# Half-product pairs of a gate/up stage extended to product 5 and to the first down part, with buffers handed out by hand

## The chip, the cores and the metric

One Trainium2 chip, one core of it. The metric is the device time of one execution in microseconds (us). The time of the kernel before is the median of three runs, 1880.92 us (1879.19 to 1881.81). One further execution was recorded by the hardware profiler: it took 1882.15 us, of which 1880.4 us lie between the first and the last instruction (the span). All rows of the profile and of the trace come from that execution.

## What is computed

One layer of a hybrid decoder, on 1024 prompt rows and 8 sample rows (1032 tokens together), in float32: an input projection, three branches (a gated linear recurrence, sliding-window attention, attention into 256 memory tokens), gates that merge them, an output projection, and at the end

```
h = layer_norm(ALPHA * x + merged @ w_out, ln1_g, ln1_b)
gt, up = jnp.split(h @ w_gate_up, 2, axis=-1)
h = layer_norm(ALPHA * h + (jax.nn.silu(gt) * up) @ w_down, ln2_g, ln2_b)
```

with D_MODEL 1024 and an inner width of 2816, which is 22 blocks of 128. The change lies in the last two lines: `h @ w_gate_up` (22 gate blocks and 22 up blocks) and the first part of the product with `w_down`.

## The kernel before, in words

**Products.** Every float32 matrix is split into a high and a low part, hi = the value rounded to the fast matmul type, lo = the rest. A matmul of two such matrices is three matmuls on TensorE: high by high, low rows by high weights, high rows by low weights (L285, L286, L287 in `fast_product`). Weights are 128x128 blocks, the moving rows are 258 tokens wide (a quarter of 1032).

**Units of seven products.** A *unit* makes 256 output columns (for the gate stage one gate block and one up block, for the down stage two row blocks) for all 1032 tokens by a Strassen scheme in its Winograd form: seven products of quarter-size matrices, numbered 0 to 6, in place of eight. Each product needs a weight sum (`fast_quarter`: an addition on VectorE at L269 for products 1, 2, 4 and 5, then the high part by a copy on ScalarE, L84, and the low part by a subtraction on VectorE, L85), and an operand sum of the activations (`ts`, made once for all units). `fast_step` issues one product: for each of two quarter columns p it has 4 k-blocks x 3 = 12 matmuls, so 24 for a product and 168 for a unit, and then takes the sums out of the banks (PSUM): products 0, 1 and 2 by ScalarE copies into small tiles (p1s, p5s, u2s; L320), products 3, 4, 5 and 6 by VectorE additions into the unit's two results za and zb (L325, L327, L330; in the down units product 6 by a ScalarE copy, L1864). Products 0, 2, 4 and 6 of a quarter column add up in one bank b, products 1 and 5 in d, so that the next product may go into the bank only when the copy of the running sum has been made.

**Units in pairs.** The gate stage has 20 units (columns 2 to 21; 0 and 1 are done in another way), taken in pairs (u, v). In the first nine pairs product 3 of both units is not made as a full product: product 3 of two units has the same operand, so that the two together are one matrix product, which is again made by seven *half products* p0, p1, p4 and p6 (p0, p1 and p4 hold two each; `second_quarter`, `second_step`). They cost 7 x 6 = 42 matmuls in place of 2 x 24 = 48, and use operand sums t2 that `second_combos` makes during the first pair. Their banks are pb, pc and pd.

**Order.** `gate_up_down` writes one list of steps, gate units first, then two *down parts* of four units each (units are named fg2 to fg21, f00 to f03, f10 to f13). Weight preparation runs three steps ahead of the products. The scheduler keeps, on each engine, an order that follows from this list, so an instruction that waits holds up all that stands behind it on its engine. The operands of a down part are loaded in the last unit of the stage before it (`down_operand`: operand i+1 after step i; it takes a free z slot, loads from the scratch f or t in DRAM, and splits into the tile that an operand of the stage before has left).

**Buffers.** Results za, zb, G, operand sums and loads for row sums are 128x1032 tiles of one pool z (10 slots, waits decided by the pool in turn); raw weights use 6 tiles, weight sums 4, split weights 5 high and 4 low. A finished gate unit is multiplied into a tile G and stored to scratch f by SP's queue; a finished down unit is added to scratch h in DRAM by two accumulating DMAs from GpSimd's queue (POOL, L1868), and its z slots are free when they have landed.

Of the kernel before, what the change touches and what calls it, by code (L numbers as in the profile page):

```python
# [60 lines left out]
class Builder:  # L61
# [124 lines left out]

    def zt(self, name):
        return self.z.tile([P, T], F32, tag="z", name=name, bufs=self.zbufs)
# [47 lines left out]
    def pair_load(self, u, st, src0, src1, other=None):  # L236

        h = D // 2
        raw = lambda j, e, src: self.half_raw(src[:, e * h:(e + 1) * h], h, f"ur{u}_{j}{e}")
        if other is not None:  # L240
            a11, a12, a21, a22 = (raw(j, e, src) for j, src in enumerate((src0, src1)) for e in range(2))
            st["second"] = raw(2, 1, other)
        else:
            a11, a21, a22, a12 = raw(0, 0, src0), raw(1, 0, src1), raw(1, 1, src1), raw(0, 1, src0)
        return {"raw": [[a11, a12], [a21, a22]], "u": u}
# [51 lines left out]
    def fast_step(self, st, i, ts, finish):  # L297
# [9 lines left out]
        for p in range(2):  # L307
# [10 lines left out]
            if i in (0, 1, 2):  # L318
# [16 lines left out]
        if st.get("pd") is not None and i == 0:  # L335
            nc.vector.scalar_tensor_tensor(st["s", 0, 1], st["pd"]["p", 1], 1.0, st["s", 0, 1], op0=ALU.mult,
                                           op1=ALU.subtract)
# [908 lines left out]
    def h_combos(self, h, ts):  # L1246
# [9 lines left out]
        for p in range(2):  # L1256
            b11, b21, b12, b22 = self.R[p, 0], self.R[p, 1], self.R[2 + p, 0], self.R[2 + p, 1]
            t1 = self.zt(f"ht1_{p}").rearrange("p (k n) -> p k n", k=4)
            tt(t1, b11, b12, ALU.subtract)
            keep(1, p, t1)  # L1260
            yield
# [6 lines left out]
            keep(6, p, b11)  # L1268
            yield
# [743 lines left out]
```

## Time and profile before

| what | value |
|---|---|
| median of three runs | 1880.92 us (1879.19 to 1881.81) |
| profiled execution | 1882.15 us, span 1880.4 us |
| mean granted TensorE clock | 0.997 |
| DVE (VectorE) busy | 1396.7 us, 74% |
| ACT (ScalarE) busy | 1058.6 us, 56% |
| DMA, mean | 164 GB/s, 308.14 MB moved |
| first gate pair fg2/fg3 | starts at 1237.6 us |

PE is TensorE, DVE VectorE, ACT ScalarE, POOL GpSimd, SP the engine that issues most DMAs. "Busy" is the time in which at least one instruction of an engine is recorded; the recorded durations of neighbours may overlap, so that what an instruction costs its engine is the distance from its start to the next one's.

### The profile page before, as it was taken

What the parts mean: (1) busy time and instruction counts of PE and PEld (TensorE: products, weight loads), DVE (VectorE), ACT (ScalarE), POOL (GpSimd) and SP (SyncE); (2) the same over time, 40 slices, a digit from 0 to 9 for tenths busy, and PEclk for the clock granted to TensorE, in tenths of its full rate; (3) what the DMA queues carried; (4) which work ended last, traced back from release to release, by engine and by line L of the source; (5) the groups of instructions that cost most, each with busy time, mean ns of one, the idle gap of its engine ahead of it and who ended that gap; (6) DMA issues with size and microseconds to landing.
All of it is one profiled execution on the core that took longest, in us unless ns stands there. A gap on an engine that the chain in (4) does not pass through costs nothing.

```text
span 1880.4 us, 37977 instructions
## 1 busy us (share of the span) xinstructions
PE 1861.4 (99%) x14670; PEld 1846.0 (98%) x14670; DVE 1396.7 (74%) x2807; ACT 1058.6 (56%) x2264; POOL 125.0 (7%) x187
## 2 busy tenths in 40 slices
PE   9999999999999999999999999999999999999998
PEld 9999999999999999999999999999999999999998
DVE  7878878888788757568787567786677667858486
ACT  6576676665666756568774234544444444635454
POOL 1001002110000000021210000000000000001100
PEclk9999999999999999999999999999999999999998
DMA  9535345447344368647535251224355345758872
GB/s 329 175 117 174 108 145 167 137 139 267 117 160 164 120 198 267 213 128 238 170 103 189 91 192 57 69 88 146 123 182 201 95 152 194 260 139 266 173 212 91
DMA packets 182213, 308.14 MB, mean 164 GB/s; under 512 B 19264, under 2 KB 97040, under 8 KB 182032
## 3 DMA queue, kind: packets, MB, share of 16 engines
q1 hardware_dynamic: 174928, 286.08, 45.9%
q0 software_dynamic: 4224, 14.78, 4.0%
q10 hardware_dynamic: 2880, 4.85, 0.7%
q8 instruction: 115, 1.88, 0.4%
q14 instruction: 66, 0.54, 0.1%
HBM read 222.10 MB, written 87.73 MB: 165 GB/s over the span
## 4 chain that ended last, share of the span: by engine, by line
PE 89%; DVE 5%; ACT 2%; DMA 2%; issue 1%; SPq 0%; POOL 0%; ACTq 0%; DVEq 0%
PE ub L285 5%; PE ub L287 5%; PE ub L286 5%; PE ubfg L286 4%; PE ubfg L287 4%; PE ubfg L285 4%; PE ud L287 2%; PE ud L286 2%; PE ud L285 2%; PE udfg L287 2%; PE udfg L285 2%; PE udfg L286 2%; PE ubf L285 2%; PE op L130 2%; PE ubf L286 2%; PE op L132 2%
## 5 line engine op out<-in xcount | busy, mean ns | idle before, releaser
L285 PE MATMUL ub<-th,u_6h 128*128 128x258 f32 x240 | 68.5, 285 | 2.7 <-DVE sq L966 1.4
L285 PE MATMUL ub<-th,u_2h 128*128 128x258 f32 x240 | 68.1, 284 | 0.7 <-ACT p1s L320 0.7
L285 PE MATMUL ub<-th,u_4h 128*128 128x258 f32 x240 | 68.2, 284 | 0.3 <-ACT u2s L320 0.3
L287 PE MATMUL ud<-th,u_5l 128*128 128x258 f32 x240 | 68.1, 284 | 0.0
L285 PE MATMUL ud<-th,u_5h 128*128 128x258 f32 x240 | 68.1, 284 | 0.0
L285 PE MATMUL ub<-th,u_0h 128*128 128x258 f32 x240 | 68.1, 284 | 0.0
L287 PE MATMUL ub<-th,u_6l 128*128 128x258 f32 x240 | 68.1, 284 | 0.0
L287 PE MATMUL ud<-th,u_1l 128*128 128x258 f32 x240 | 68.1, 284 | 0.0
L287 PE MATMUL ub<-th,u_4l 128*128 128x258 f32 x240 | 68.0, 284 | 0.0
L287 PE MATMUL ub<-th,u_2l 128*128 128x258 f32 x240 | 68.0, 284 | 0.0
L287 PE MATMUL ub<-th,u_0l 128*128 128x258 f32 x240 | 68.0, 283 | 0.0
L285 PE MATMUL uc<-th,u_3h 128*128 128x258 f32 x240 | 68.0, 283 | 0.0
L285 PE MATMUL ud<-th,u_1h 128*128 128x258 f32 x240 | 68.0, 283 | 0.0
L287 PE MATMUL uc<-th,u_3l 128*128 128x258 f32 x240 | 68.0, 283 | 0.0
L286 PE MATMUL ub<-tl,u_6h 128*128 128x258 f32 x240 | 67.7, 282 | 0.0
L286 PE MATMUL ub<-tl,u_0h 128*128 128x258 f32 x240 | 67.6, 282 | 0.0
L286 PE MATMUL ud<-tl,u_5h 128*128 128x258 f32 x240 | 67.6, 282 | 0.0
L286 PE MATMUL ud<-tl,u_1h 128*128 128x258 f32 x240 | 67.6, 282 | 0.0
L286 PE MATMUL ub<-tl,u_4h 128*128 128x258 f32 x240 | 67.6, 282 | 0.0
L286 PE MATMUL ub<-tl,u_2h 128*128 128x258 f32 x240 | 67.6, 282 | 0.0
L286 PE MATMUL uc<-tl,u_3h 128*128 128x258 f32 x240 | 67.6, 282 | 0.0
L130 PE MATMUL op<-mh,woh 128*128 128x258 f32 x224 | 63.4, 283 | 0.0
(1034 smaller groups left out, 8207.2 us busy)
## 6 DMA issues: line engine op xcount, KB each, us to landing
ur<-win SPq DMA_DIRECT2D x120, 256.0 KB, 3.4
urfg<-wgu SPq DMA_DIRECT2D x89, 256.0 KB, 3.0
scr_f<-G SPq DMA_DIRECT2D x22, 516.0 KB, 2.8
f<-scr_f SPq DMA_DIRECT2D x16, 516.0 KB, 4.0
fs<-scr_t SPq DMA_DIRECT2D x16, 516.0 KB, 5.1
dck<-cmk SPq DMA_DIRECT2D x32, 256.0 KB, 4.6
dcv<-cmvT SPq DMA_DIRECT2D x32, 256.0 KB, 4.6
urf<-wdn SPq DMA_DIRECT2D x32, 256.0 KB, 3.1
```

The costliest lines, as they stand in the source:

```text
L130: nc.tensor.matmul(ps, sh, mh, start=opens and i == 0, stop=False)
L132: self.last_mm = nc.tensor.matmul(ps, sl, mh, start=False, stop=closes and i == last).ins
L285: mm(sh[:, w], xh, start=opens and k == 0, stop=False)
L286: mm(sh[:, w], xl, start=False, stop=False)
L287: self.last_mm = mm(sl[:, w], xh, start=False, stop=k == 3).ins
```

## The change

- **More pairs with half products for product 3.** All ten gate pairs and the two pairs of the first down part now replace product 3 of both units by p0, p1, p4, p6 (twelve pairs, before nine). The operand sums for the down part are made by `down_sums`, kept in a new scratch t2 and loaded by `second_load`.
- **Product 5 in the same way, in the first nine gate pairs** ("fifth"): product 5 of both units becomes the half products v0, v1, v4 and v6. Their operand sums are made once (`fifth_combos`), stored to a new scratch t5 and loaded again in every pair (four loads of 516 KB into two buffers, `fifth_load`). v4 and v6 of a pair are issued inside the next pair, behind its product 0 and product 1.
- **Order in a pair.** In a fifth pair p4 stands straight behind (v, 0), and p6 behind (v, 1); before, p4 stood behind (v, 1) and p6 behind (v, 4). In fifth units the running sum of product 2 goes into za by a VectorE addition in place of the ScalarE copy u2s.
- **Buffers by hand.** z slots (8 in this stage, 10 around it), raw weight tiles and sum tiles are handed out from queues and put back when the program is done with them; a raw load is issued when a tile is put back. G is made in place in za.
- **Down operands.** `down_operand` now runs with operand i after step i (before, i+1), into the tile of the operand with the same number (`home = i`), and puts its z slot back at once.

The core of the diff:

```diff
-        order, cut = [], 2 * ((NF - 2 - PLAIN) // 2)
+        where = {u: n for n, u in enumerate(units)}
+        pairs = [n for n in range(0, len(units), 2) if units[n][0] != FAST - 1]
+        second = {units[n + e] for n in pairs for e in range(2)}
+        fifth = [n for n in pairs if units[n + 1][0] == "g" and units[n + 1][1] < NF - 1]
+        order, tail = [], []
         for n in range(0, len(units), 2):
-            steps = [(units[n + e], i) for e in range(2) for i in range(7)]
-            if n < cut:
-                u, v = units[n:n + 2]
-                steps = [(u, 0), (u, 1), (u, "p0"), (u, 2), (u, 4), (u, "p1"), (u, 5), (u, 6),
+            u, v = units[n:n + 2]
+            if n in fifth:
+                steps = [(u, 2), (u, "p0"), (u, 4), (u, "p1"), (u, 6), (v, 0), (v, "p4"), (v, 1), (v, "p6"), (v, 2),
+                         (v, "v0"), (v, 4), (v, "v1"), (v, 6)]
+            elif u in second:
+                steps = [(u, 2), (u, "p0"), (u, 4), (u, "p1"), (u, 5), (u, 6),
                          (v, 0), (v, 1), (v, "p4"), (v, 2), (v, 4), (v, "p6"), (v, 5), (v, 6)]
-            order += steps
+            else:
+                steps = [(u, i) for i in range(2, 7)] + [(v, i) for i in range(7)]
+            order += [(u, 0)] + tail[:1] + [(u, 1)] + tail[1:] + steps
+            tail = [(v, "v4"), (v, "v6")] if n in fifth else []
...
-        sums, seconds = deque(), self.second_combos()
+        sums, seconds = deque(), chain(self.second_combos([self.R[p, 1] for p in range(2)]), self.fifth_combos())
...
+            if where[u] // 2 * 2 in fifth and where[u] % 2:
+                for j in {0: (1,), "p4": (2,), "v1": (4, 6)}.get(i, ()):
+                    self.fifth_load(j)
...
-                if u[1] == last[u[0]][1] - 1 and i == 3:
-                    self.down_operand(nxt, 0, moving[nxt])
-                if u == last[u[0]] and i < 6:
-                    while sums:
-                        for _ in sums.popleft():
-                            pass
-                    self.down_operand(nxt, i + 1, moving[nxt])
+            if nxt < FAST and u == last[u[0]]:
...
+                if i == "p6":
+                    self.down_operand(nxt, 3, moving[nxt])
+                    if nxt < FAST - 1:
+                        self.second_load(nxt)
+                elif i == "v4":
+                    self.down_operand(nxt, 5, moving[nxt])
+                elif not isinstance(i, str):
+                    self.down_operand(nxt, i, moving[nxt])
```

```diff
+    def fifth_combos(self):
...
+        def put(j, src, sign=1.0):
+            t = self.zt(f"t5{j}")
+            pair = t.bitcast(F32R)[:, :2 * QN], t.bitcast(F32R)[:, 2 * QN:]
+            (self.split if sign > 0 else partial(self.split_scaled, scale=sign))(*pair, src)
+            nc.sync.dma_start(self.scr["t5"][:, (1, 2, 4, 6).index(j), :], t)
+            self.zfree(t)
...
+    def fifth_step(self, su, sv, j, ts, fu, fv):
...
+            z, sign = {0: (za[:, 0], 1.0), 3: (za[:, 0], 1.0), 2: (za[:, 1], 1.0), 5: (za[:, 1], 1.0), 1: (zb[:, 1], -1.0),
+                       4: (zb[:, 1], -1.0), 6: (zb[:, 0], -1.0)}[i]
+            stt(z, ps, sign, z, op0=ALU.mult, op1=ALU.add)
```

Three places in the engines' orders follow. L numbers of the changed kernel are its own (L302 is L269 of before, L328 to L330 are L285 to L287, L367 is L320, L374 is L327, L383 is L336).

VectorE in the first gate pair, before: from the first split of an operand sum (t2l3) to the low weights of product 1 of unit fg2 (ufg2_1l). R are activations, usfg2 weight sums.

```order
L85 TENSOR_TENSOR t2l30_16605<-R11_15174,t2h30_16604 128x516
L1317 TENSOR_TENSOR R01_14872<-R11_15174,R01_14872 128x516
L1287 TENSOR_TENSOR G1_16303<-ft1_3_16509,fu1_3_16511 128x258
L85 TENSOR_TENSOR t2l20_16603<-R11_15174,t2h20_16602 128x516
L269 TENSOR_TENSOR usfg2_1_16556<-urfg2_10_16546,urfg2_11_16548 128x512
L96 SCALAR_TENSOR_TENSOR t2l20_16603<-R01_14872,t2h20_16602 128x516
L269 TENSOR_TENSOR usfg2_2_16566<-usfg2_1_16556,urfg2_00_16542 128x512
L85 TENSOR_TENSOR ufg2_1l_16559<-usfg2_1_16556,ufg2_1h_16558 128x512
```

The same stretch of the changed kernel; z are slots (z2 holds the first sum for product 5), s0 to s2 sum tiles, raw0 to raw2 raw weights.

```order
L85 TENSOR_TENSOR t2l30_16609<-z3_14869,t2h30_16608 128x516
L1338 TENSOR_TENSOR z9_14878<-ft1_3_16509,fu1_3_16511 128x258
L85 TENSOR_TENSOR t2l20_16607<-z3_14869,t2h20_16606 128x516
L1369 TENSOR_TENSOR z1_14867<-z3_14869,z1_14867 128x516
L1394 TENSOR_TENSOR z7_14873<-z5_14871,z7_14873 128x516
L1374 TENSOR_TENSOR z1_14867<-z1_14867 128x516
L96 SCALAR_TENSOR_TENSOR t2l20_16607<-z1_14867,t2h20_16606 128x516
L85 TENSOR_TENSOR z2_14868<-z7_14873,z2_14868 128x516
L302 TENSOR_TENSOR s0_16542<-raw1_16547,raw2_16548 128x512
L302 TENSOR_TENSOR s2_16544<-raw0_16546,raw1_16547 128x512
L302 TENSOR_TENSOR s1_16543<-s0_16542,raw0_16546 128x512
L85 TENSOR_TENSOR ufg2_1l_16564<-s0_16542,ufg2_1h_16563 128x512
```

Four rows more stand between the two, and a fifth (L1393, 128x516) stands ahead of the low weights of product 0, where before there was none; the weight sum of product 1 is now the fourth row from the end.

VectorE around p4, before (pair fg6/fg7; L336 reads bank pd, L1380 and L1382 take p4 out):

```order
L85 TENSOR_TENSOR ufg6_p4l_17826<-usfg6_p1_17682,ufg6_p4h_17825 128x512
L269 TENSOR_TENSOR usfg8_2_18107<-usfg8_1_18040,urfg8_00_17892 128x512
L85 TENSOR_TENSOR ufg7_2l_17858<-usfg7_2_17855,ufg7_2h_17857 128x512
L269 TENSOR_TENSOR usfg7_2_17855<-usfg7_2_17855,urfg7_01_17641 128x512
L85 TENSOR_TENSOR ufg7_4l_17907<-usfg7_4_17904,ufg7_4h_17906 128x512
L336 SCALAR_TENSOR_TENSOR p1sfg7_1_17889<-pdfg6_17693,p1sfg7_1_17889 128x258
L269 TENSOR_TENSOR usfg8_4_18153<-urfg8_00_17892,urfg8_10_17896 128x512
L85 TENSOR_TENSOR ufg6_p6l_17941<-urfg7_01_17641,ufg6_p6h_17940 128x256
L1380 SCALAR_TENSOR_TENSOR zafg7_17950<-pbfg6_17691,p1sfg7_1_17889 128x258
```

In the changed kernel (pair fg4/fg5; L383, L1537 and L1539 are the same three operations):

```order
L85 TENSOR_TENSOR ufg5_1l_17284<-s1_16543,ufg5_1h_17283 128x512
L85 TENSOR_TENSOR ufg4_p6l_17314<-raw4_16550,ufg4_p6h_17313 128x256
L85 TENSOR_TENSOR ufg5_2l_17353<-s3_16545,ufg5_2h_17352 128x512
L302 TENSOR_TENSOR s3_16545<-s3_16545,raw4_16550 128x512
L383 SCALAR_TENSOR_TENSOR p1sfg5_1_17345<-pdfg4_17219,p1sfg5_1_17345 128x258
L1421 TENSOR_TENSOR s1_16543<-s3_16545 128x256
L1537 SCALAR_TENSOR_TENSOR z2_14868<-pbfg4_17217,p1sfg5_1_17345 128x258
```

The reader of pd now stands two rows behind the low weights of (v, 2), with p4 due straight behind (v, 0); on TensorE the scheduler puts 6 to 10 matmuls of (v, 1) between the first and the second product of p4.

SP's queue around the load of operand 3 of the second down part, before; the waits are the semaphores of the row (DMASW are those of GpSimd's accumulating DMAs; 2 and 3 belong to unit f01, 4 and 5 to unit f02).

```order
L1429 DMA fs120_22587<-scr_t_80 128x1032 [waits DMAHW3_49,DMASW0_49]
L1429 DMA fs121_22593<-scr_t_80 128x1032 [waits DMAHW4_49,DMASW1_49]
L1391 DMA f1TrueFalse0_22632<-scr_f_79 128x4x258 [waits DMAHW5_49,DMASW2_49]
L1391 DMA f1TrueFalse1_22638<-scr_f_79 128x4x258 [waits DMAHW6_49,DMASW3_49]
L105 DMA urf11_00_22844<-wdn 128x512 [waits DMAHW7_49,DVE_49]
```

The changed kernel; operand 3's second half is the load into z3.

```order
L1610 DMA z0_14866<-scr_t_80 128x1032 [waits DMAHW6_49,DVE_49]
L1549 DMA z3_14869<-scr_f_79 128x4x258 [waits DMASW4_49]
L1610 DMA z1_14867<-scr_t_80 128x1032 [waits DMAHW0_49,DVE_49]
L261 DMA raw4_16550<-wdn 128x512 [waits DMAHW1_49,DVE_49]
L1610 DMA z5_14871<-scr_t_80 128x1032 [waits DMAHW2_49,Activation_49]
L261 DMA raw5_16551<-wdn 128x512 [waits DMAHW3_49,DVE_49,Activation_49]
```

What waited for a DMA of unit f01 now waits for one of unit f02, the unit just before f03 in the order. ScalarE's queue at the same place, among the copies u2s that free bank b of f03, before (dth13_0 is the split of operand 3's first half):

```order
L320 ACTIVATE p5sf03_1_22585<-udf03_1_22572 128x258
L84 CAST uf03_6h_22644<-urf03_11_22284 128x512
L320 ACTIVATE u2sf03_0_22616<-ubf03_0_22501 128x258
L84 CAST dth13_0_22634<-f1TrueFalse0_22632 128x1032
L320 ACTIVATE u2sf03_1_22630<-ubf03_1_22516 128x258
```

The changed kernel; d13h11 is the split of the load into z3.

```order
L367 ACTIVATE p5sf03_1_22476<-udf03_1_22463 128x258
L84 CAST uf03_5h_22509<-s3_16545 128x512
L84 CAST uf03_6h_22552<-raw5_16551 128x512
L84 CAST d13h11_22610<-z3_14869 128x1032
L367 ACTIVATE u2sf03_0_22526<-ubf03_0_22400 128x258
L95 ACTIVATE dth12_0_22543<-z4_14870 128x1032
L367 ACTIVATE u2sf03_1_22540<-ubf03_1_22415 128x258
```

The cast stands ahead of both copies u2s of f03; before, the split of operand 3 (dth13_0) stood between the two, and its load waited for unit f01 alone.

More of the change, by code (lines that the diff above doesn't have):

```diff
@@ L234, in combos, with ask, raw_loads, raw_done @@
             yield cost
[L236 to L245, printed above, removed]
+    def ask(self, u, st, n, src):
+        self.rwait.append((f"ur{u}_{n}", st, n, src))
+    def raw_loads(self):
+        while self.rwait and self.rfree:
+            name, st, n, src = self.rwait.popleft()
+            t = st["r"][n] = self.rfree.popleft()
+            self.last_load = self.nc.sync.dma_start(t, src).ins
+    def raw_done(self, st, *keys):
+        for n in keys:
+            self.rfree.append(st["r"].pop(n))
+        self.raw_loads()
     def fast_load(self, u, src0, src1, staged=False):
@@ L1334, in second_quarter @@
         elif j == 1:
-            src, z = (self.w1.tile([P, D // 2], F32, tag="sum", name=f"us{su['u']}_p{e}", bufs=4) for e in range(2))
+            src, z = (self.sum_tile() for e in range(2))
             add(src[:, lo], b[:, lo], b[:, hi])
@@ L1483, in quarter @@
             else:
                 self.fast_quarter(st[u], i)
-        load(0)
+                if i == 4 and st[u]["fifth"]:
+                    self.fast_quarter(st[u], 5)
+        h = D // 2
+        self.rwait = deque()
+        self.rfree = deque(self.wpool.tile([P, h], F32, tag="raw", name=f"raw{i}", bufs=6) for i in range(6))
+        for n, u in enumerate(units):
+            st[u] = {"u": f"f{u[0]}{u[1]}", "r": {}, "fifth": n // 2 * 2 in fifth, "first": n % 2 == 0}
+            st[u]["opens"] = u in second and (n % 2 == 0 or st[u]["fifth"])
+            src = {10 * (j + 1) + e + 1: a[:, e * h:(e + 1) * h] for j, a in enumerate(rows(u)) for e in range(2)}
+            for k in (11, 21, 22) if u in second and n % 2 else (11, 21, 22, 12):
+                self.ask(st[u]["u"], st[u], k, src[k])
+            if u in second and n % 2 == 0:
+                self.ask(st[u]["u"], st[u], "v", rows(units[n + 1])[0][:, h:])
@@ L1715, in last_products @@
                         self.residual(0, 1, ((2, 4),))
-                        for part in ((1, 0), (1, 1), (2, 0), (2, 1), (3, 0), (3, 1)):
-                            self.residual(*part)
+                        self.rest = deque((q, kh) for q in (1, 2, 3) for kh in range(2))
+                while self.rest and self.zslots:
+                    with self.tc.issue_after(self.last_load):
+                        self.residual(*self.rest.popleft())
                 ps = self.bank(("mm", "s")[m % 2], f"dl{m}_{q}")[:, :QN]
@@ L1859, in __init__ @@
     def __init__(self, b, part, j):
-        self.b, self.rows = b, (2 * j, 2 * j + 1)
+        self.b, self.rows, self.ends = b, (2 * j, 2 * j + 1), (part, j) == (FAST - 1, 3)
     def late(self, dst, ps):
```

311 lines of the change are left out of this document (239 added, 72 removed).

## The prediction

> **What bounds the kernel now.** I read the page's busy times first, then TensorE's waits in the stretch that the change touches, then the windows, which give the rate.
>
> ```profile
> span 1880.4 us, 37977 instructions
> PE 1861.4 (99%) x14670; PEld 1846.0 (98%) x14670; DVE 1396.7 (74%) x2807; ACT 1058.6 (56%) x2264; POOL 125.0 (7%) x187
> L285 PE MATMUL ub<-th,u_6h 128*128 128x258 f32 x240 | 68.5, 285 | 2.7 <-DVE sq L966 1.4
> ```
>
> TensorE is busy all the time, so a matmul less is time less, unless a wait comes in its place. The mean of 285 ns for a matmul is not its price, because matmuls overlap; the price is the distance between starts. Here are windows of the first two gate pairs (span, then busy time and count of PE, PEld, DVE, ACT, POOL, then clock and DMA):
>
> ```profile
> 1237.60:1277.20 39.60, 39.60 (x329) 39.50 (x328) 32.12 (x61) 19.07 (x38) 0.00 (x0) 1.00 0.45 147
> 1277.20:1316.80 39.60, 39.60 (x331) 39.60 (x330) 26.44 (x47) 16.85 (x34) 0.00 (x0) 1.00 0.36 120
> ```
>
> 331 matmuls in 39.6 us are 0.12 us each. From 1100 to 1800 us TensorE waits once:
>
> ```profile
> PE fg L138 <- ACT hh L84: 0.5, 1, 0.5
> ```
>
> So before, every weight sum, bank copy and load of the stage is hidden. DVE is the next engine, with 26.44 of 39.6 us in the steady pair.
>
> The profiled execution took 1882.15 us, 1.23 above the median of 1880.92; I sum against the former and carry the difference over to the median. A difference under 0.2% (3.8 us) can't be told from no change here.
>
> **The change part by part.** *1. Fewer matmuls: -8.6 us.* A pair of full products is 48 matmuls, seven half products 42. Product 5 in nine pairs saves 9 x 6 = 54, product 3 in three further pairs 3 x 6 = 18; 72 x 0.12 = 8.6 us. A steady pair falls from 330 matmuls (39.6 us) to 324 (38.9).
>
> *2. First gate pair: +3.6 us (2.9 to 4.2).* DVE runs without a gap here while the operand sums are made:
>
> ```profile
> 1238.10 0.42 DVE L1287 TENSOR_TENSOR G<-ft,fu 128x258 f32<-128x258 f32 x1
> 1238.43 0.69 DVE L85 TENSOR_TENSOR t2l<-R,t2h 128x516 fp32r<-128x516 f32 x1
> 1239.04 0.69 DVE L269 TENSOR_TENSOR usfg<-urfg,urfg 128x512 f32<-128x512 f32 x1
> 1239.64 0.69 DVE L96 SCALAR_TENSOR_TENSOR t2l<-R,t2h 128x516 fp32r<-128x516 f32 x1
> 1240.24 0.69 DVE L269 TENSOR_TENSOR usfg<-usfg,urfg 128x512 f32<-128x512 f32 x1
> 1240.85 0.69 DVE L85 TENSOR_TENSOR ufg_1l<-usfg,ufg_1h 128x512 fp32r<-128x512 f32 x1
> ```
>
> Start to start a row of 512 or 516 elements takes 0.605 us, one of 258 takes 0.33. ufg_1l ends at 1241.54. TensorE meets it here:
>
> ```profile
> 1240.49 0.33 PE L285 MATMUL udfg<-hth,ufg_1h 128*128 128x258 f32 x1
> 1241.03 0.32 PE L1369 MATMUL pbfg<-hh,ufg_p0h 128*128 128x258 f32 x1
> 1241.59 0.39 PE L287 MATMUL udfg<-hth,ufg_1l 128*128 128x258 f32 x1
> ```
>
> Four matmuls with the high weights fill 1240.49 to 1241.03, four of p0 the rest; nothing is lost. In the changed order five more rows stand ahead of ufg2_1l, of 512 or 516 elements each: 5 x 0.605 = 3.0, so it ends near 1244.55. p0 no longer stands in between, so the matmul that needs it could start at 1240.49 + 4 x 0.12 = 1240.97: a wait of 3.6 us. (Most of it falls ahead of ufg2_1h already, since its sum s0 is late as well.) The low bound takes four rows off by one short one, the high adds a row that falls late. DVE has time to catch up in the rest of the pair: 32.12 us of work in 39.6 before.
>
> *3. p4 straight behind (v, 0): +0.9 us (0 to 2).* The second half of p4 goes into bank pd, which VectorE must have read (L383, in before L336), and that needs ScalarE's copy of the second column of (v, 0). The chain in a pair of before:
>
> ```profile
> 1300.56 0.29 PE L287 MATMUL ubfg<-hh,ufg_0l 128*128 128x258 f32 x1
> 1300.95 0.69 DVE L85 TENSOR_TENSOR ufg_4l<-usfg,ufg_4h 128x512 fp32r<-128x512 f32 x1 [1.48 <-PE ubfg L287]
> 1301.07 0.38 ACT L320 ACTIVATE p1sfg<-ubfg 128x258 f32<-128x258 f32 x1
> 1301.56 0.42 DVE L336 SCALAR_TENSOR_TENSOR p1sfg<-pdfg,p1sfg 128x258 f32<-128x258 f32 x1
> 1301.90 0.68 DVE L269 TENSOR_TENSOR usfg<-urfg,urfg 128x512 f32<-128x512 f32 x1
> ```
>
> From the last start of (v, 0) the split on DVE starts 0.39 later. In the changed order that split (ufg5_2l), one addition and then L383 follow: 0.39 + 0.6 + 0.6 + 0.42 = 2.0 us. TensorE has 6 matmuls of p4's first half and 6 to 10 of (v, 1) to put in: 13 to 17 starts, 1.6 to 2.0 us. So 0 to 0.4 us, taken as 0.1 in nine pairs. It costs nothing where DVE's addition runs in time that is free, and 0.2 a pair where all have 6 matmuls as filler.
>
> *4. DVE in the steady pairs: 0 (0 to 1).* A fifth pair adds four additions of 256 (1.3 us), splits for v0, v1, v4 and v6 (2.1), seven additions out of the new banks (2.35) and four for product 2 (1.35), and drops two splits (1.2) and four additions of product 5 (1.35): +4.6 us. 26.44 + 4.6 = 31.0 of 38.9 us is 80%. A row for a stretch in which DVE has no time left bounds it:
>
> ```profile
> 500.00:520.00 20.00, 19.05 (x159) 18.84 (x158) 19.08 (x45) 10.62 (x20) 2.21 (x3) 1.00 0.58 204
> 520.00:540.00 20.00, 19.94 (x165) 19.66 (x165) 19.83 (x38) 12.88 (x27) 0.00 (x0) 1.00 0.54 195
> ```
>
> Even at 95% and more TensorE loses 0 to 1 us in 20; at 80% the queue has room, and I take nothing. If the room is not where it is needed (rows of one product that wait for a bank), up to 0.1 us a pair. The four t5 loads a pair bring 2.1 MB, 54 GB/s, on top of 120; the tightest is issued when v1's first half has left its buffer, with 6 + 24 + 24 = 54 matmuls (6.5 us) until v4 needs it, and a load of that size lands in about 4 (fs, below), so it is hidden.
>
> *5. Gate stage to first down part: +0.4 us (0 to 2).* Operands are loaded one step later, with the t2 loads beside them. Before, this boundary was DVE-bound without a wait of TensorE:
>
> ```profile
> 1628.00:1648.00 20.00, 20.00 (x168) 20.00 (x168) 19.97 (x27) 15.57 (x25) 0.00 (x0) 1.00 0.69 252
> ```
>
> A step is 24 matmuls, 2.9 us, so only what was ready by less than that ahead of its use is late now. 0.4 is one row of 258 on DVE too late, 2.0 a loss of 10% in the window; with DVE full but TensorE never short before, I take the small end.
>
> *6. First to second down part: +3.1 us (0 to 8.4).* The load of operand 3 into z3 waits until GpSimd's accumulation of f02's zb has landed, and its cast on ScalarE stands ahead of the copies u2s of f03, for which product 4 of f03 waits. Rows of before, from the first matmul behind a unit (time 0 of the chain) to the issue, then the transfers and the cast:
>
> ```profile
> 1676.21 0.28 PE L285 MATMUL ubf<-d00h,uf_0h 128*128 128x258 f32 x1
> 1677.62 0.87 POOL L1868 DMA_DIRECT2D scr_h<-zbf  x1 [2.34 <-ACT zbf L1864]
> 1697.91 1.06 ACT L84 CAST d11h<-fs 128x1032 fp32r<-128x1032 f32 x1 [0.54 <-PE ubf L286]
> 1698.88 0.38 ACT L320 ACTIVATE p1sf<-ubf 128x258 f32<-128x258 f32 x1
> ```
> ```profile
> scr_h<-zaf POOLq DMA_DIRECT2D x8, 516.0 KB, 6.3
> scr_h<-zbf POOLq DMA_DIRECT2D x8, 516.0 KB, 7.8
> fs<-scr_t SPq DMA_DIRECT2D x8, 516.0 KB, 4.0
> ```
>
> Issue at 1.4; 6.3 to land (the first of its two, as zaf was before); 4.0 for the load; 0.97 for the cast, 0.4 for the copy: 13.1. Product 4 of f03 is due after three full products and one p4, 84 x 0.12 = 10.1 (as p4 and p6 are now in the part 0 too). So 3.0 to 3.1 us. Ends: the shortest landing in the row of the tile, and the transfers of the crowded stretch 1676 to 1705:
>
> ```profile
> DMA to landing us min/median/max: 5.4/7.0/10.5
> scr_h<-zbf POOLq DMA_DIRECT2D x2, 516.0 KB, 8.5
> urf<-wdn SPq DMA_DIRECT2D x6, 256.0 KB, 7.2
> ```
>
> With 5.4 and 2.7 (a smaller load's) it is 10.9, and any other work of TensorE hides it: 0. With 8.5 and 7.2 it is 18.5: 8.4. I take the middle, as rows of the same size say.
>
> [...]
>
> *7. The last stage* has the same steps with other buffers: 0 (up to 1 either way).
>
> Sum: -8.6 + 3.6 + 0.9 + 0.4 + 3.1 = -0.6 us. 1882.15 - 0.6 = 1881.55 for a profiled execution, 1880.92 - 0.6 = 1880.3 for the median.
>
> **The rivals.** *A. The boundary hides itself (faster).* If scr_h lands in about 5 us or the scheduler's filler reaches past the chain, terms 5 and 6 are 0; if DVE is quick enough for p4, term 3 too. Then -8.6 + 3.6 = -5.0: 1875.9. For it: the shortest landing of 5.4, and that TensorE never waited here before. Against: what waited for f01 now waits for f02, a unit (168 matmuls, 20 us) later. Chance 0.33.
>
> *B. The wait for the accumulation is a long one (slower).* The DMA queues were at their limit at this boundary before (8.5 and 7.2 us), and the loads of the next part fall into it again. With 18.5 us, term 6 is 8.4: -8.6 + 3.6 + 0.9 + 0.4 + 8.4 = +4.7: 1885.6. It decides from a chain of some 17.6 us, where term 6 passes 7.5. Chance 0.18.
>
> *C. The clock drops in the new waits (slower).* At the end of the kernel TensorE runs dry:
>
> ```profile
> 1868.00:1872.00 4.00, 3.16 (x33) 2.87 (x31) 1.19 (x4) 1.50 (x5) 0.00 (x0) 0.85 0.48 161
> 1872.00:1876.00 4.00, 1.05 (x5) 0.82 (x4) 2.91 (x7) 2.45 (x5) 0.00 (x0) 0.50 0.20 66
> ```
>
> With 1.05 of 4 us busy the clock goes to 0.50. If the waits of 3.6 and 3.1 us both do this, and 4 us then run at half clock, each costs 2 us more: -0.6 + 4 = +3.4: 1884.3, and over the bound as soon as a wait is half a microsecond longer than in the sum. Against: the wait of term 2 is split in two by four matmuls. [...] Chance 0.03.
>
> *D. The matmuls count 285 ns each:* 72 x 0.285 = 20.5, 1868 with the waits. The windows exclude it; under 0.01.
>
> **How the numbers follow.** The forecast, within 0.2%, has 0.46; faster 0.33 (A); slower 0.21 (B and C). The time is the forecast's, 1880.3. The range takes in A with the low bound of term 2 (-5.7, 1875.2) and B with half of its excess left out; 1874.5 to 1887.0.
>
> **What would show it.** In the changed profile: 14404 PE rows less the filler, with 324 matmuls in 38.9 us of a steady pair; about 3.6 us of waiting ahead of ufg2_1h and ufg2_1l; about 0.1 us a pair at p4, on L383; 3 us at f03 on ACT u2s (L367), with the cast of d13h ended by a DMA; the clock at 1.00 through. The forecast is wrong if the pairs don't shrink by 0.7 us each, if the first pair's wait is under 2 us, or if the boundary's is 0 or over 7.

## The result, and the profile after

| | median | runs |
|---|---|---|
| before | 1880.06 us | 1878.78 to 1881.81 (4) |
| after | 1892.00 us | 1890.91 to 1893.39 (4) |

The change makes the kernel slower by 0.63%: the ratio is 1.0063 (95% interval 1.0046 to 1.0081), some 12 us. The forecast was 1880.3 with a range up to 1887.0; both are wrong. The profiled execution of after took 1893.39 us.

The head of the page after:

```profile
span 1891.7 us, 38154 instructions
PE 1861.8 (98%) x14598; PEld 1841.5 (97%) x14598; DVE 1453.2 (77%) x2967; ACT 1059.1 (56%) x2260; POOL 123.5 (7%) x187
```

There are 72 matmuls fewer (14670 to 14598), exactly as counted, and the busy time of PE stays where it was (1861.4 and 1861.8 us), which says again that busy time isn't the price of a matmul. To see where the time is, I take one stretch that holds all of the change but the last stage: from the first matmul of fg2 to the first one of f13. As a window it is, in before and in after (columns as in the prediction):

```profile
1237.61:1777.22 539.61, 539.61 (x4484) 539.51 (x4483) 375.36 (x628) 247.40 (x477) 16.49 (x19) 1.00 0.55 170
```
```profile
1236.70:1788.31 551.61, 538.43 (x4412) 534.56 (x4411) 431.68 (x788) 250.34 (x474) 16.45 (x19) 0.99 0.69 212
```

551.61 - 539.61 = 12.0 us: the whole loss lies here, and the last stage adds nothing. TensorE was busy in all 539.61 us before; now 551.61 - 538.43 = 13.2 us are idle. So 72 x 0.12 = 8.6 us were gained and 12.0 + 8.6 = 20.6 us came back. Its start also moves: 1237.61 and 1236.70 here, 1233.61 to 1238.39 in the experiments below, which are the same up to there. So I judge experiments by the length of the stretch in the profiled run, and by the ratio of the medians.

TensorE's waits of after from 1100 to 1800 us (total, times, longest; the last four, of 0.2 to 0.5, left out), where before had one, of 0.5:

```profile
PE pdfg L1526 <- DVE p1sfg L383: 3.4, 2, 2.5
PE ubf L328 <- ACT u2sf L367: 2.9, 2, 2.3
PE udfg L328 <- ACT ufg_1h L84: 2.7, 1, 2.7
PE pbf L1526 <- DVE p1sf L1530: 1.3, 1, 1.3
PE ubf L328 <- ACT z L2091: 1.1, 1, 1.1
PE ubfg L328 <- ACT u2sfg L367: 0.5, 1, 0.5
...
```

The third line is the wait of the first pair that the prediction had, the second the one at f03. The first line is of another kind: p4's wait on L383 should cost 0.1 us in each of nine pairs, and here two pairs have 3.4 us between them. The fourth, at f00, and the fifth, at f10, are more than was forecast there (0.4 us and nothing). A steady pair and the first pair in windows:

```profile
1318.19:1357.50 39.31, 39.30 (x327) 39.10 (x326) 29.84 (x59) 16.38 (x32) 0.00 (x0) 1.00 0.52 172
1236.70:1278.92 42.22, 39.15 (x309) 38.53 (x308) 38.47 (x75) 18.48 (x37) 0.00 (x0) 0.96 0.54 183
```

The steady pair takes 39.31 us, 0.42 less than before (39.73 between the same rows, 1317.29 to 1357.02) where 0.7 was due. In the first pair the clock is 0.96 on average. In steps of 2 us:

```profile
1244.00:1246.00 2.00, 2.00 (x12) 2.00 (x11) 2.00 (x4) 0.89 (x3) 0.00 (x0) 0.53 0.86 265
1246.00:1248.00 2.00, 2.00 (x13) 2.00 (x13) 1.86 (x5) 0.32 (x2) 0.00 (x0) 0.62 0.46 180
```

From 1.7 us behind the end of the wait TensorE gets half its clock: 12 and 13 matmuls are recorded in 2 us, where at 0.12 us each there would be 17. (2 x 0.47 + 2 x 0.38) / 0.5 = 3.4 us at half clock, so 1.7 us are lost; this is an estimate from the clock, and the starts, 0.215 us apart from 1244.17 to 1247.40, give 1.5. The same comes once more at f03, from 1715.14, 0.4 us ahead of the end of the wait there:

```profile
1716.00:1720.00 4.00, 4.00 (x26) 4.00 (x26) 3.69 (x5) 3.33 (x6) 0.00 (x0) 0.68 1.01 253
```

The wait of 2.5 us at p4, in pair fg12, has its cause on VectorE's own row of instructions:

```profile
1457.06 0.43 DVE L85 TENSOR_TENSOR ufg_p6l<-raw,ufg_p6h 128x256 fp32r<-128x256 f32 x1 [0.30 <-PE ubfg L330]
1461.45 0.70 DVE L1583 TENSOR_TENSOR z<-z 128x516 f32<-128x516 f32 x1 [3.97 <-DMA z<-scr_f]
...
1462.80 0.68 DVE L85 TENSOR_TENSOR ufg_2l<-s,ufg_2h 128x512 fp32r<-128x512 f32 x1
1463.40 0.42 DVE L383 SCALAR_TENSOR_TENSOR p1sfg<-pdfg,p1sfg 128x258 f32<-128x258 f32 x1
```

L1583 and L1584 belong to `down_sums`, the operand sums for the down part, which nobody needs soon. The scheduler has put them ahead of L383, and the operand of L1583 is still being loaded: VectorE stands for 3.97 us with nothing to do, and L383, for which TensorE's p4 waits, stands behind it. The other wait on L383, in pair fg16, has the same cause:

```profile
1541.69 1.23 DVE L1563 TENSOR_TENSOR z<-z,z 128x1032 f32<-128x1032 f32 x1 [3.16 <-DMA z<-scr_f]
1542.84 0.42 DVE L383 SCALAR_TENSOR_TENSOR p1sfg<-pdfg,p1sfg 128x258 f32<-128x258 f32 x1
```

In all, rows of `down_sums` wait for loads five times in the gate stage of after, 11.6 us together. In before they did so four times, 5.7 us together and 1.9 at most, and TensorE waited for none of it.

### The profile page after: what moved, and what is told of

Read it like the earlier page. It is cut to its first block, busy times and chain, and to the rows that moved or that the text cites. A ratio compares the mean times of both kernels' runs of the same rounds, so it can differ in the third digit from the quotient of the medians.

```text
span 1891.7 us, 38154 instructions
## 1 busy us (share of the span) xinstructions
PE 1861.8 (98%) x14598; PEld 1841.5 (97%) x14598; DVE 1453.2 (77%) x2967; ACT 1059.1 (56%) x2260; POOL 123.5 (7%) x187
## 4 chain that ended last, share of the span: by engine, by line
PE 80%; DVE 8%; DMA 7%; ACT 3%; issue 2%; SPq 0%; POOL 0%; ACTq 0%; DVEq 0%
PE ub L328 5%; PE ub L330 5%; PE ub L329 5%; PE ubfg L328 4%; PE ubfg L330 4%; PE ubfg L329 4%; PE ud L330 2%; PE ud L329 2%; PE ud L328 2%; DMA z<-scr_f 2%; PE brs L141 2%; PE brs L138 2%; PE brs L139 2%; PE bra L141 1%; PE bra L138 1%
## 5 line engine op out<-in xcount | busy, mean ns | idle before, releaser
L328 PE MATMUL ub<-th,u_6h 128*128 128x258 f32 x240 | 68.5, 285 | 1.5 <-DVE zb L374 1.1
L328 PE MATMUL uc<-th,u_3h 128*128 128x258 f32 x240 | 68.1, 284 | 0.7 <-ACT v L497 0.7
L328 PE MATMUL ub<-th,u_4h 128*128 128x258 f32 x240 | 68.2, 284 | 0.2 <-ACT u2s L367 0.2
L330 PE MATMUL ud<-th,u_5l 128*128 128x258 f32 x240 | 68.1, 284 | 0.0
L328 PE MATMUL ud<-th,u_5h 128*128 128x258 f32 x240 | 68.1, 284 | 0.0
L328 PE MATMUL ub<-th,u_0h 128*128 128x258 f32 x240 | 68.1, 284 | 0.0
L330 PE MATMUL ub<-th,u_6l 128*128 128x258 f32 x240 | 68.1, 284 | 0.0
L330 PE MATMUL ub<-th,u_4l 128*128 128x258 f32 x240 | 68.1, 284 | 0.0
L330 PE MATMUL ud<-th,u_1l 128*128 128x258 f32 x240 | 68.1, 284 | 0.0
L330 PE MATMUL ub<-th,u_0l 128*128 128x258 f32 x240 | 68.1, 284 | 0.0
L330 PE MATMUL ub<-th,u_2l 128*128 128x258 f32 x240 | 68.1, 284 | 0.0
L328 PE MATMUL ud<-th,u_1h 128*128 128x258 f32 x240 | 68.0, 283 | 0.0
L330 PE MATMUL uc<-th,u_3l 128*128 128x258 f32 x240 | 68.0, 283 | 0.0
L328 PE MATMUL ub<-th,u_2h 128*128 128x258 f32 x240 | 68.0, 283 | 0.0
L2095 POOL DMA_DIRECT2D scr_h<-z x16 | 14.4, 938 | 753.1 <-ACT z L2091 694.1
```

The lines of the kernel that those rows point to most:

```text
L328: mm(sh[:, w], xh, start=opens and k == 0, stop=False)
L330: self.last_mm = mm(sl[:, w], xh, start=False, stop=k == 3).ins
L2095: self.b.nc.gpsimd.dma_start(self.b.scr["h"][:, m, :], z, accum_op=ALU.add)
```

## The experiments

Three theories went into them. **Order:** VectorE's queue stands behind rows that wait for a load, or behind sums not needed yet. **Load:** VectorE simply has too much to do. **Boundary:** TensorE waits for operands of the next part, and these for the slots whose accumulation must land. `issue_after(x)` in the edits queues the instructions of a block behind instruction x on x's own engine; it takes no semaphore away. Each kernel is after with the edit shown; "stretch" is the one taken above (551.61 us in after), and each ratio is to before, in runs taken side by side.

**e1_first: the first pair's operand sums behind the low weights of product 1.**

```diff
+            if i == 1:
+                low = self.last_lo
...
-            next(seconds, None)
+            with self.tc.issue_after(low) if n > 2 else nullcontext():
+                next(seconds, None)
```

The same is done for the weight sums and row sums of the first eight steps.

> The changed kernel with VectorE's order in the first gate pair pinned: everything traced behind the weights of products 0 to 2 of unit fg2 (the last operand sum for product 3, the sums for product 5, the row-sum reductions, the weight sum of product 4) is queued behind the low weights of product 1 (ufg2_1l). Nothing is left out. Theory (order): ufg2_1l comes about 3.0 us earlier, the wait of 2.9 + 0.6 us ahead of product 1 shrinks to about 1.2 us, and with it the stretch of 3.4 us at half clock behind it (1.7 us lost) goes: -3.9 us, about 1888.1. Rival (load): VectorE is simply full here, the same rows have to run before TensorE gets on, and the wait only moves behind product 1: 1891 to 1892.

Ratio 1.0041 (1.0026 to 1.0056), stretch 547.8 us; the first pair falls from 42.22 to 40.74.

```profile
PE udfg L328 <- ACT ufg_1h L84: 1.9, 1, 1.9
```

So the sums put ahead of ufg2_1l do cost time, but 1.9 us of wait stay, and the half clock came behind a gap of only 2.1 us between starts: 37.1 us for 309 matmuls and 2.0 for the gap leave 1.6 of the 40.74. The rest of the wait isn't due to these rows. The first pair gives back 1.5 us where 3.9 were expected. That the median (1885.87 us) is even below the theory's 1888.1 is luck: the rest lies in places that the edit doesn't touch.

**e2_sums: the rows of `down_sums` at their place in the program.**

```diff
+                with self.tc.issue_after(self.last_lo):
+                    if next(sums[0], self) is self:
+                        sums.popleft()
```

> The changed kernel with VectorE's part of the down operand sums (down_sums) queued behind the last low weights traced at its place in the program, so that the scheduler can't put them ahead of the reader of bank pd (L383) in earlier steps. Nothing is left out. Theory (order): the waits of 2.6 us in pair fg12 and 1.1 us in pair fg16 ahead of p4, and the 0.6 us ahead of them at product 6 of fg12, go, because VectorE no longer stands in front of a load that has not landed: -4.2 us, about 1887.8. Rival (load): the loads of these blocks are late because the slots and the DMA queues are short, the sums then wait later, and TensorE with them: within 1 us of 1892.

Ratio 1.0031 (1.0020 to 1.0043), stretch 543.05 us, 8.6 less than after. Of the 8.6, 5.3 lie in the gate pairs behind the first and 2.4 in f00/f01. The other 0.9 is a balance of pairs that the edit doesn't touch; in f02/f03 the wait is as long as in after (2.5 us), but brought no half clock this time: the mean clock is 0.96 in the first pair, as in after, but 1.00 over the stretch, in after 0.99. The medians differ by 5.9 us (1886.09, from 1881.73 to 1889.79 in nine runs, of which the profiled one was the fastest). What is left of the list of waits (two more are of 0.5 and 0.2):

```profile
PE udfg L328 <- ACT ufg_1h L84: 2.7, 1, 2.7
PE ubf L328 <- ACT u2sf L367: 2.5, 1, 2.5
PE ubf L328 <- ACT z L2093: 1.7, 1, 1.7
...
```

```profile
1233.66:1776.71 543.05, 535.86 (x4412) 532.90 (x4411) 432.36 (x788) 249.57 (x474) 16.51 (x19) 1.00 0.69 215
```

Every wait on L383, L374, L1530 and on p6 is gone, and each of the eight gate pairs between the first and the last takes 39.30 us. VectorE does the same work in this stretch as in after (788 rows, 432.36 against 431.68 us). So it was the order and not the load: the same rows, a few places later, cost nothing. It also removed the waits at f00, 2.4 us, which I had not put down to order.

**e3_pd: nothing of (v, 2) ahead of L383.**

```diff
+            self.pd_read = nc.vector.scalar_tensor_tensor(st["s", 0, 1], st["pd"]["p", 1], scale, st["s", 0, 1], ...).ins
...
+                with self.tc.issue_after(self.pd_read) if i == "p4" else nullcontext():
+                    quarter(*order[n + ahead])
```

> The changed kernel with the weights of (v, 2) queued on VectorE behind the reader of bank pd (L383), in all twelve pairs. Nothing is left out. Theory (order): the gap of 0.27 us at the second half of p4 in every fifth pair closes, 9 x 0.27 = -2.4 us, about 1889.6; the long waits in fg12 and fg16 stay, since what blocks there is a load. Rival: the gap is the latency from ScalarE's copy through VectorE's read, which no order changes: 1892.

Ratio 1.0062 (1.0047 to 1.0077): not to be told from after. In the trace the edit shows. p4's second half in after, where it waits until L383 is done, and in e3_pd:

```profile
1342.18 0.42 DVE L383 SCALAR_TENSOR_TENSOR p1sfg<-pdfg,p1sfg 128x258 f32<-128x258 f32 x1
...
1342.37 0.28 PE L328 MATMUL udfg<-hth,ufg_1h 128*128 128x258 f32 x1
1342.65 0.38 PE L1526 MATMUL pdfg<-hh,ufg_p4h 128*128 128x258 f32 x1
1342.88 0.28 PE L1527 MATMUL pdfg<-hl,ufg_p4h 128*128 128x258 f32 x1
```
```profile
1339.48 0.28 PE L330 MATMUL udfg<-hth,ufg_1l 128*128 128x258 f32 x1
1339.62 0.39 PE L1526 MATMUL pdfg<-hh,ufg_p4h 128*128 128x258 f32 x1
1339.85 0.28 PE L1527 MATMUL pdfg<-hl,ufg_p4h 128*128 128x258 f32 x1
```

In after the two starts are 0.28 and 0.23 apart where 0.12 is the mean of a steady pair: 0.27 us a pair. In e3_pd 0.14 and 0.23: 0.16 a pair is gone, and steady pairs take 39.15. In nine pairs that is 1.4 us, less than the other waits vary between runs: at product 6 (L374) TensorE waits 2.7 us here and 0.2 in after. The long waits at p4 stay (2.8 us in two pairs), as they must if their cause is `down_sums`.

**e4_pin: the boundary's operand splits behind the weights and copies that stand ahead of them in the program.**

```diff
+                with self.tc.issue_after(self.last_lo), self.tc.issue_after(self.last_copy):
                     if i == "p6":
                         self.down_operand(nxt, 3, moving[nxt])
```

> The changed kernel with the splits of the down operands (down_operand, second_load) queued on ScalarE behind the last bank copy and on VectorE behind the last low weights traced at their place in the program; the cast d13h11 then stands behind both copies u2s of f03. Nothing is left out. Theory (order): the wait of 2.6 us at product 4 of f03 and the 3.4 us at half clock behind it (1.7 us lost) go, -4.3 us, about 1887.7; the waits at f00 and f10 (2.6 and 1.4 us) may change by a microsecond either way. Rival (transfer): the load into z3 lands too late for product 3 of f10 and its bank copies anyway, so that the wait moves to f10: at most -1.5 us, 1890.5 or more.

Ratio 1.0099 (1.0082 to 1.0116): worse than after, stretch 556.6 us. The wait at f03 is gone, and a longer one stands at f10, with the clock at half in the window around its end:

```profile
PE ubf L328 <- ACT z L2092: 4.9, 1, 4.9
```
```profile
1728.00:1732.00 4.00, 2.56 (x12) 2.57 (x13) 4.00 (x6) 4.00 (x8) 0.47 (x1) 0.50 0.98 389
```

Here order is no cure. Behind the four operand loads that follow f02's accumulation, the next ones leave SP at 1721.37 us, in after at 1718.24, with a DMA share near 1 (0.98 in the window above, 1.01 in that of after from 1716 to 1720): what was late at f03 is later at f10. That the later splits hold the slots back, and so these loads, is argued from this and not shown by a run of its own.

**e5_slots: the two t5 tiles serve as z slots in the down parts.** They are handed out by hand too, join the z queue at (f00, 0), and leave it in the second part.

```diff
+            if (u, i) == ((0, 0), 0):
+                self.zslots.extend(self.t5free)
```

> The changed kernel with the two tiles that held the sums for product 5 (free once the gate stage is over) handed out as z slots during the down parts, ten in place of eight, so that the operand 3 of the second down part goes into them and no longer waits for GpSimd's accumulation of f02; its casts then stand behind both copies u2s of f03 by themselves. Nothing is left out. Theory (slot): the wait of 2.6 us at product 4 of f03, the 1.7 us lost at half clock behind it and the 1.4 us at f10 go: -5.7 us, about 1886.3. Rival (transfer, as the pinned order of the earlier run suggests): another load on the same queue still waits for that accumulation, everything behind it is late, and the wait comes back at f10: 1889 to 1891.

Ratio 1.0050 (1.0037 to 1.0064). The pair f02/f03 is whole (39.67 us for 330 matmuls, 3.8 less than in after), but:

```profile
PE ubf L328 <- ACT z L2098: 3.6, 1, 3.6
```

Two more slots only move the accumulation's wait to another load, which stands in the same queue on SP.

**e6_first: all sums of the first pair behind ufg2_1l**, with `n < 8` in place of `n > 2` in the edit of e1_first.

> The changed kernel with all operand sums for products 3 and 5 and the reductions of the first gate pair queued on VectorE behind the low weights of product 1 (ufg2_1l), so that six rows of 516 elements fewer stand ahead of them than in the earlier run on this place. Nothing is left out. Theory: 6 x 0.605 = 3.6 us more than cover the 2.1 us of wait that the earlier run left; no wait, so no stretch at half clock: the first pair from 42.2 to 37.1 us, -5.1 us, about 1886.9. Rival: the operand sums are now too late for p1, and TensorE waits there for what it didn't wait for at product 1: first pair over 40 us, 1890 or more.

Ratio 1.0044 (1.0030 to 1.0058); the first pair takes 40.72, as in e1_first, in another way:

```profile
PE udfg L328 <- ACT ufg_1h L84: 1.6, 1, 1.6
PE pdfg L1528 <- DVE ufg_p1l L85: 0.4, 1, 0.4
PE pbfg L1526 <- DVE z L1537: 0.4, 1, 0.4
```

1.6 at product 1, then new waits of 0.4 at p1 and p6, where VectorE is late with what was pushed back. 37.1 us for 309 matmuls and 2.4 of waits leave 1.2 us, too little for a stretch at half clock like that of after (1.5 to 1.7). Here VectorE's load does show: in the first pair of after it has 38.47 us of work in 42.22.

**e7_all: the cures together** (e6_first, e2_sums, e3_pd, e5_slots).

> The changed kernel with four cures together: the first pair's sums behind ufg2_1l, the down sums pinned at their place, the weights of (v, 2) behind the reader of bank pd, and the two tiles for product 5 as z slots in the down parts. Nothing is left out. Theory (each wait is an order or a slot, not load): the stretch from the first gate pair to the last unit, 543.1 us with the down sums pinned alone, loses 4.8 (first pair), 1.4 (p4) and 4.2 (f03 and f10): 532.7, against 539.6 in the kernel before: about 1873, -0.37%. Rival (load): VectorE with about 5 us more work a pair has no room once TensorE runs without waits, and half of what is saved comes back: 1878 to 1882, no measurable gain on the kernel before.

Ratio 1.0011 (1.0002 to 1.0020), stretch 541.2 us. The median, 1882.31 us, is near the rival's time, but not for its reason: with no waits left the steady gate pairs take 39.13 us, so VectorE has the room. The loss is at f10:

```profile
PE ubf L328 <- ACT z L2105: 4.3, 1, 4.3
```

**e8_fetch: operands of the second down part fetched one step earlier, in the order of their use**, with the slots of e5_slots; the slots of f02's results are kept out of the queue until the second part begins, so that no load waits for that accumulation.

```diff
+            early = {((0, 2), 6): 0, ((0, 3), 0): 1, ((0, 3), 1): 2, ((0, 3), 2): 4, ((0, 3), 4): 3, ((0, 3), "p6"): 5,
+                     ((0, 3), 5): 6}.get((u, i))
...
+                self.fetched[1, early] = [self.fetch(1, early, p) for p in range(2)]
...
+        elif self.rows[0] == 4 and FAST - 1 > self.part:
+            self.b.late = za, zb
```

> The changed kernel with ten z slots in the first down part as in the earlier run on slots, and besides: the operands of the second down part are fetched one step before they are split, in their own order on the queue, and the two slots of f02's results are put back only when the second part begins, so that no operand waits for the accumulation of f02. Nothing is left out. Theory (slot): the waits at f03 and f10 both go; the pair f02/f03 from 43.5 to 39.7 us, the pair f10/f11 from 41.8 to 40.4, -5.2 us, about 1886.8. Rival (transfer): the queues are at their limit there whatever waits for what, landings stay at 8 us and more, and 3 us or more of wait remain in the two pairs together.

Ratio 1.0048 (1.0033 to 1.0063). f02/f03 takes 39.67 us, f10/f11 43.27: the wait at f10 is 2.6 us in place of the 3.6 of e5_slots. The accumulation has nothing left to hold up, yet a wait remains, in windows with a DMA share of 0.87 and 1.06:

```profile
1704.00:1708.00 4.00, 4.00 (x36) 4.00 (x35) 4.00 (x5) 3.99 (x9) 0.00 (x0) 1.00 0.87 232
...
1712.00:1716.00 4.00, 4.00 (x36) 4.00 (x35) 4.00 (x6) 4.00 (x6) 0.00 (x0) 1.00 1.06 192
```

**e8_first: p0 of the first pair back in its old place**, behind product 1 and ahead of product 2.

```diff
+            if not n:
+                steps[:2] = steps[1::-1]
```

> The changed kernel with p0 of the first gate pair alone back at its old place, straight behind product 1 and ahead of product 2. Nothing is left out. Theory (VectorE's order, the sum s0 and ufg2_1h are late): p0 gives TensorE a few matmuls more ahead of ufg2_1l, but its own weights come behind ufg2_1l on VectorE, and the wait of 2.9 us ahead of ufg2_1h stays: first pair 41.5 to 42.2 us, at most -0.7. Rival (missing filler): the place of p0 was what hid the wait before, and most of the 5.1 us go: first pair 38 to 39 us.

Ratio 1.0052 (1.0036 to 1.0068), first pair 41.79 us in place of 42.22:

```profile
PE udfg L328 <- ACT ufg_1h L84: 2.7, 1, 2.7
```

The wait has its old length. The place of p0 alone isn't the cause; the sums ahead of the weights are.

**e9_all: e8_first's order, e1_first, e2_sums, e3_pd and e8_fetch**.

> The changed kernel with all cures: down sums pinned, the weights of (v, 2) behind the reader of bank pd, p0 of the first pair at its old place with the later sums behind ufg2_1l, and the operands of the second down part fetched early into slots that don't wait for f02. Nothing is left out. Theory: from the run with four cures (541.2 us from the first gate pair to the last unit) 6 us go at f10 and 1 to 2 in the first pair: 533 to 534, against 539.6 in the kernel before, about 1874, -0.3%. Rival (load): the wait at f10 comes back elsewhere in the down parts: 1879 or more, no gain on the kernel before.

Ratio 0.9991 (0.9982 to 1.0000), stretch 537.9 us. The first pair is at 38.12 us: order and sums together do what neither did alone. The gap between starts is 1.26 us, 0.9 less than in e1_first, and the other 1.7 us are the half clock that e1_first had and this run has not: 37.1 us for the matmuls leave 1.0, no more than the gap. One long wait stays, at f10 (2.7 us on L2128; with half clock behind it, put at 1.7, these are 4.4 of the 4.6 us by which the stretch of e10_all is shorter). ScalarE there:

```profile
1707.40 1.06 ACT L84 CAST d15h<-z 128x1032 fp32r<-128x1032 f32 x1 [2.52 <-DMA z<-scr_f]
1710.07 1.05 ACT L84 CAST d15h<-z 128x1032 fp32r<-128x1032 f32 x1 [1.61 <-DMA z<-scr_f]
...
1711.55 0.38 ACT L2128 ACTIVATE z<-ubf 128x258 f32<-128x258 f32 x1
```

It is the pattern of `down_sums` on another engine: two casts of an operand that isn't needed yet wait 2.52 and 1.61 us for their loads (issued at 1699.19 and 1700.94, so 8 and 9 us under way), and the copy L2128, which frees TensorE's bank, stands behind them.

**e10_all: e9_all, with the casts of operands 5 and 6 queued behind the copies of f03's product 6.**

```diff
+                elif nxt == FAST - 1 and i == 6:
+                    with self.tc.issue_after(self.last_copy):
+                        self.down_operand(nxt, 5, moving[nxt])
+                        self.down_operand(nxt, 6, moving[nxt])
```

> The changed kernel with all cures of the last run, and besides the splits of operands 5 and 6 of the second down part queued on ScalarE behind the copies of product 6 of f03, for which product 0 of f10 waits. Nothing is left out. Theory (what is left is ScalarE's queue standing behind a load): the 2.7 us of wait at f10 and the 1.7 us at half clock go, the stretch from the first gate pair to the last unit from 537.9 to 533.5 us, against 539.6 in the kernel before: about 1874, -0.3%. Rival (transfer): the loads of operands 5 and 6 land too late for f10's products 2 and 3 as well, and 2 us or more of wait remain in the pair f10/f11: 1877 or more, within 0.2% of the kernel before.

Ratio 0.9967 (0.9955 to 0.9980): 1874.52 us (1871.33 to 1876.75, 6 runs) against 1879.8 for before. This version beats both kernels. Its waits and its stretch:

```profile
PE udfg L328 <- ACT ufg_1h L84: 1.0, 1, 1.0
PE fg L138 <- ACT hh L84: 0.5, 1, 0.5
```
```profile
1238.39:1771.65 533.26, 532.28 (x4412) 531.36 (x4411) 430.99 (x788) 250.24 (x473) 16.51 (x19) 1.00 0.70 219
1315.62:1354.76 39.14, 39.14 (x326) 39.08 (x325) 30.61 (x61) 16.40 (x32) 0.00 (x0) 1.00 0.56 181
```

With the same 788 rows on VectorE and the same matmuls the stretch is 18.35 us shorter than in after (551.61 to 533.26), and the granted clock is 1.00, over the stretch and in its first pair (38.07 us), f02/f03 and f10/f11. Against before (539.61) that is 6.3 of the 8.6 us that the fewer matmuls were to bring. The steady pair (second line) has VectorE at 30.61 of 39.14 us, 78%.

## Why the prediction was wrong

The terms as forecast and as the runs show them, against the length of the stretch. A pair's loss is its duration less 0.12 us for each matmul, after less before:

| term | forecast | found | from |
|---|---|---|---|
| 1 fewer matmuls | -8.6 | -8.6 | x4484 to x4412 |
| 2 first gate pair | +3.6 | +5.2 | 3.5 of waits, 1.7 of half clock |
| 3 p4 | +0.9 | +2.4 | 9 x 0.27 |
| 4 DVE in steady pairs | 0 | +5.3 | e2_sums, gate pairs |
| 5 gate to first down part | +0.4 | +2.4 | e2_sums, f00 |
| 6 first to second down part | +3.1 | +5.2 | 3.84 at f02/f03, 1.34 at f10 |
| sum | -0.6 | +11.9 | measured 12.0 |

**The step that failed first is term 4**, "at 80% the queue has room, and I take nothing". The room is there: 29.84 of 39.31 us is 76%, and 78% in e10_all without a loss. But with that room too VectorE's rows ran in the order of their queue (L383 at 1463.40 us, behind L1583 at 1461.45), and I priced the rows that the change adds (how many, how long) without asking what each of them waits for and who stands behind it. A row of 0.7 us that waits 3.97 us for its operand costs its engine 4.7. The bound I took, a stretch in which DVE is busy at 95%, answers the load theory and says nothing on this. e2_sums settles it: with the order of these rows alone changed, the gate pairs lose nothing to them any more, 5.3 us less than in after. That a load held them is shown in pairs fg12 and fg16. Not shown is why they cost nothing in before, where such rows waited for loads too: the waits were shorter there, and p4 stood one product later, and no run separates the two.

**Term 5** failed by the same step. I took the boundary for a question of DVE being full and gave it the small end; e2_sums removes the 2.4 us with DVE no less full (34.27 us busy in the 39.87 of f00/f01, in after 32.38 in 42.27). By which path the order acts there stays open: in after ScalarE's casts of operands 3 and 5 waited 0.97 to 1.21 us for their loads, and in e2_sums they don't.

**Term 2 was right in mechanism, and its wait in size** (3.5 of 3.6 us, as the loss of 5.2 less the half clock; 3.06 of it stand as waits in the rows below), in the place that was named: first ahead of ufg2_1h, then a little ahead of ufg2_1l.

```profile
1242.40 0.39 PE L328 MATMUL udfg<-hth,ufg_1h 128*128 128x258 f32 x1 [2.66 <-ACT ufg_1h L84]
1243.56 0.39 PE L330 MATMUL udfg<-hth,ufg_1l 128*128 128x258 f32 x1 [0.40 <-DVE ufg_1l L85]
```

What was mis-sized is the cost of the clock behind it, **rival C**, at 0.03. C's chain was right, 1.7 and 1.5 us where it had 2 each, and it came at both places. My reason against it, that the wait is split in two, was no reason: a gap of 2.1 us between starts was enough in e1_first (1.6 us lost beside it).

**Term 6 was right in mechanism**, and its links can be read off: the accumulation, the load that waits for it, and ScalarE.

```profile
1704.39 0.86 POOL L2095 DMA_DIRECT2D scr_h<-z  x1 [19.25 <-ACT z L2091]
...
1709.77 0.37 SPq L1549 DMA_DIRECT2D z<-scr_f  x1
...
1714.16 1.05 ACT L84 CAST d13h<-z 128x1032 fp32r<-128x1032 f32 x1 [2.94 <-DMA z<-scr_f]
1715.11 0.38 ACT L367 ACTIVATE u2sf<-ubf 128x258 f32<-128x258 f32 x1
```

Issue to the load's issue 5.4 us (6.3 forecast), to the cast 4.4 (4.0), to the copy 0.95 (0.97). The wait is 2.3 us and not 3.1, and half clock makes up the other 1.5 of the 3.84. The landing of 5.4 is close to the 5 us on which rival A was built, and the wait came all the same: with the sum's other links 5 us still leave 1.7 us of wait, so this condition of A did not carry its conclusion. Beyond f03 the prediction had nothing, and 1.3 us fell there: e4_pin, e5_slots and e7_all show that this boundary passes a wait on to f10 as soon as f03 is freed of it.

**Term 3** was 0.27 in each pair where 0.1 was forecast. The wait for L383 is 0.16 of it (e3_pd); the other 0.11, between the first and second matmul of that half of p4, stays in e3_pd and e10_all, and its cause stays open.

**Rival B** had the right sign, and 4.7 of the 12 us, for a wrong cause: no single wait was as long as it asked for, there were many.

Two slips in the prediction's figures change nothing in this. Its 14404 PE rows should read 14670 - 72 = 14598, as measured, and the top of its range, 1887.0, leaves out no part of rival B, which it puts at 1885.6.

## What to carry to other kernels

Price an added instruction by what it waits for and who stands behind it on its engine, not by its duration and its engine's share of busy time: VectorE was 76% busy, and still 7.7 us were lost by the order of its rows. Where this boundary was short of transfers, moving one consumer back passed the wait on (4.9 us at f10 in e4_pin, 3.6 in e5_slots); it went only when loads left earlier in the order of use and nothing urgent stood behind their first readers (e10_all). And a cure that shows nothing alone (e3_pd, e8_first) may be needed beside the others, so read its own place in the trace before dropping it.

## What the hardware showed beyond that

- **Waits of 1.9 to 4.9 us brought half clock, but not all of them did.** The two half-clock stretches of after between 1100 and 1800 us last 3.41 us each (1244.10 to 1247.51 and 1715.14 to 1718.55, at 0.50). In e4_pin it was longer: 0.50 from 1728 to 1732 and 0.68 in the 4 us behind. The half clock came with waits of 1.9 us (e1_first), 2.7 and 2.3 us (after), 4.3 us (e7_all, 0.89 and 0.69 in the two windows from 1712 to 1720) and 4.9 us (e4_pin); it did not come with 2.5 us in pair fg12 of after or 2.5 us at f03 in e2_sums. How little TensorE did in such a stretch doesn't decide it alone either. Here are 3.41 us of after up to each of the two falls, and 3.41 us with the wait in fg12:

```profile
1240.69:1244.10 3.41, 1.29 (x8) 1.08 (x9) 3.41 (x7) 2.20 (x6) 0.00 (x0) 1.00 0.60 207
1711.73:1715.14 3.41, 1.48 (x13) 1.26 (x11) 1.09 (x3) 0.98 (x2) 0.86 (x1) 1.00 1.02 324
1460.30:1463.71 3.41, 1.12 (x10) 0.90 (x8) 2.22 (x4) 0.43 (x2) 0.00 (x0) 1.00 0.14 54
```

TensorE is busy for 1.29 and 1.48 us ahead of the falls. In the third row it is busy for less, 1.12 us, and the clock stays at 1.00 behind it (1.00 over the whole pair, 1439.59 to 1479.07). What decides isn't shown by these runs.
- **Two loads took twice as long where the DMA share was 1.05.** A load of 516 KB took 4.0 us in the row fs<-scr_t of before (the median of eight, 1640 to 1730 us). Two in e9_all took 8 and 9 us from issue to the cast that waited for them, in this window among others (1.07 in the 4 us ahead of it, 0.93 in those behind):

```profile
1704.00:1708.00 4.00, 4.00 (x35) 4.00 (x35) 4.00 (x7) 1.48 (x3) 0.00 (x0) 1.00 1.05 359
```

That the share is the cause no run of its own shows.
